# A hybrid decoder layer: v transposed on TensorE, the head's mean taken out on VectorE, and other figures in the list scheduler

## The chip, the cores and the metric

The kernel runs on one core of a Trainium2 chip. The core has five engines, each with its own instruction queue worked through in order: TensorE (PE in the profile; its weight loads are shown apart as PEld), VectorE (DVE), ScalarE (ACT), GpSimd (POOL) and SyncE (SP), which here issues all DMA transfers. PE writes to PSUM, whose banks hold 128 x 512 f32 each; POOL and DMA do not reach PSUM here. The metric is the device time of one execution in microseconds (us); lower is better.

## The reference

One layer of a decoder trunk with 4096 positions and a width of 1024. A normalised input is projected to the inputs of two groups of heads; both groups' outputs are gated, concatenated and projected back, then a residual and a final norm follow. The part that matters here is the second group, eight RWKV-7 heads of 64 channels.

```python
def _rwkv7_scan(r, decay, k, v, kk, a):
    def step(S, inp):
        r_t, w_t, k_t, v_t, kk_t, a_t = inp
        sa = jnp.einsum('bhvk,bhk->bhv', S, -kk_t)
        S = (S * w_t[:, :, None, :]
             + sa[..., None] * (kk_t * a_t)[:, :, None, :]
             + v_t[..., None] * k_t[:, :, None, :])
        y = jnp.einsum('bhvk,bhk->bhv', S, r_t)
        return S, y
...
    y = _rwkv7_scan(r_h, decay.reshape(hs), k_h, v_h, kk, a.reshape(hs))
    mu = jnp.mean(y, axis=-1, keepdims=True)
    var = jnp.mean(jnp.square(y - mu), axis=-1, keepdims=True)
    y = ((y - mu) * lax.rsqrt(var + RWKV_GN_EPS)).reshape(B, T, RWKV_W)
    y = y * rwkv_ln_w.astype(f32) + rwkv_ln_b.astype(f32)
    bonus = jnp.sum(r_h * k_h * rwkv_r_k.astype(f32), axis=-1, keepdims=True) * v_h
    rwkv_out = (y + bonus.reshape(B, T, RWKV_W)) * jax.nn.silu(rg)
```

The state is linear in v, row by row of the value dimension. So the mean of y over a head's 64 value channels is removed by removing the mean of v over those channels before the recurrence; the kernel does it there. The bonus uses v with its mean.

## The kernel before, in words

Activations lie with channels on the 128 partitions and time along the free axis, in eight blocks of 512 positions. The projections are f16 products: activations and weights are each split into a high and a low half, and three products of the halves are summed, so that a 128-channel output over 512 positions takes 24 products of 128 x 512.

Eight blocks times four pairs of heads make 32 **units**, numbered from 0. For each unit `rwkv_ab` projects k, r, v and the gate; builds decays; and makes the triangular products of eight chunks of 64 positions in two groups of four (tile `bank<-DD,bk` in the profile, a form that fills 64 of the 128 rows of the PE array). Masked copies put them into DD and Nb. For the inverse of the triangular factors, the 32 x 32 diagonal blocks of Nb go through DRAM (`nd`, then `f`), POOL makes 31 pairs of a product and a sum (`tm`, `Tc`), and the result returns through DRAM (`td`) into Nb. For the last unit DVE does that work. `rwkv_i` completes the 64 x 64 inverses with small products (`Ta`, `Nb`). `rwkv_c` runs the recurrence over the eight chunks: three products into the bank `ch`, with copies on ACT (`us`, `uv`) and the state's update on DVE (`sv`, `Sst`) between them. The output products go to the bank `y`, and `rwkv_d` scales them. DD and Nb have two buffers each, so the decay products of a unit wait until the recurrence two units earlier is done (`done["CC"] >= u - 1`).

At the end of `rwkv_ab`, v (channels by time) is brought to time by channels: four products per unit with the constant `c64` as the moving operand. `c64` holds identity minus 1/64 in a block for each head, so the product transposes and removes the head's mean at once. Four ACT copies take the bank into `sv`, which has two buffers.

The gated linear attention (`gla_lr`, `gla_proj`, `gla_pair`), the norm of the input (`x_block`), the splitting of weights in the first blocks (`split_w`, `split_o`) and the output projection (`out_block`, `out_last`) are further streams. Weights are split once, kept in DRAM (`wdr`) and loaded again for each block on the SP queue, together with every other transfer.

**The order** is made by the program. The streams are run against a model of the engines (`account`) that records every instruction as a `Step` with its duration, the delay until others see its result (`lag`) and its dependences (`put`). Then a list scheduler goes forward and backward over all steps (`forward`, `backward`) up to thirteen times and keeps the order with the smallest modelled end. The instructions are then issued to each engine's queue in that order, which the chip cannot change. The figures that stand in the model are these: a result is seen by another engine 0.2 us after its end (0.25 from PE), and by the same engine 0.075, 0.1 or 0.18 sooner (DVE, ACT, POOL); a DMA issue holds the SP queue for 0.63 us and its transfer starts 1.28 us after; a POOL instruction on n elements of two operands takes 0.14 + n x 2.13/960; a load's data are there 1.6 us after its transfer, plus `SPARE` of 0.45. Among the next twelve PE steps, one that keeps the form of the array tile (rows by columns) is preferred by 2.0 us over another, and a change of form is modelled with 0.09 us.

All instructions are recorded by one helper, so they all carry its line (L408) in the profile; they are told apart by their tiles.

Of the kernel before, what the change touches and what calls it, by code (L numbers as in the profile page):

```python
# [10 lines left out]
F32 = mybir.dt.float32  # L11
# [4 lines left out]
ALU = mybir.AluOpType  # L16
AX = mybir.AxisListType
PSUM = bass.MemoryType.PSUM
DRAM = bass.MemoryType.DRAM

P = 128
# [4 lines left out]
SPARE = 0.45  # L26
# [45 lines left out]
CK_C64 = 64  # L72
# [9 lines left out]
def hymba_kernel(ctx, tc, xT, wt, wg, wo, wua, gup, pk, ck, out):  # L82
# [5 lines left out]
    one = ctx.enter_context(tc.tile_pool(name="one", bufs=1))  # L88
# [14 lines left out]
    ready, used, busy = {}, {}, {}  # L103
# [59 lines left out]
    array = Array()  # L163

    def account(eng, out, ins, d, lag, cols=0, tiles=None):
        rdy = lambda k: (lambda r: r[0] - (r[1] == eng) * {"V": 0.075, "S": 0.1, "G": 0.18}.get(eng, 0.0))(ready.get(k, (0.0, "")))
        t = max([0.0] + [rdy(k) for a in ins for k in parts(a)]
                + [used.get(k, 0.0) for k in parts(out)]
                + [rdy(k) for k in parts(out) if eng != "T"])
        if eng == "T":  # L170
            t0, d = array.put(max(t, now[0]), d, cols, tiles)
            t, now[0] = t0, array.free
        else:
            if eng == "D":
                t0 = place("H", t, 0.63)
                t = t0 + 1.28
            t = place(eng, t, d)
            if eng != "D":
                t0 = t
        for a in ins:  # L180
            for k in parts(a):
                used[k] = max(used.get(k, 0.0), t + d + (0.95 if eng == "D" else 0.1))
        for k in parts(out):
            ready[k] = (t + d + lag, eng)
        return t0

    table = [0]
    steps, wkey, rkey, wlast, readers = [], {}, {}, {}, {}
# [22 lines left out]
    def put(t0, eng, d, lag, cols, tiles, tab, outs, ins, f):  # L211

        keys = lambda aps: {k: k in {y for x in aps for y in parts(x)} for a in aps for k in whole(a)}
        ki, ko = keys(ins), keys(outs)
        for k in list(ki) + list(ko):
            t0 = max(t0, wkey.get(k, 0.0))
        for k in ko:
            t0 = max(t0, rkey.get(k, 0.0))
        s = Step(len(steps), t0, eng, d, lag, cols, tiles, tab, f)
        got = lambda m: m.lag + SPARE * (m.eng == "D") - (m.eng == eng) * {"V": 0.075, "S": 0.1, "G": 0.18}.get(eng, 0.0)  # L220
        for k, timed in ki.items():
            rkey[k] = max(rkey.get(k, 0.0), t0)
            if k in wlast:
                s.follow(wlast[k], got(wlast[k]) if timed else None)
        for k, timed in ko.items():
            wkey[k] = t0
            if k in wlast:
                s.follow(wlast[k], got(wlast[k]) if timed and eng != "T" else None)
            for m in readers.get(k, ()):
                s.follow(m, (0.95 + SPARE if m.eng == "D" else 0.1) if timed else None)  # L230
            wlast[k], readers[k] = s, []
        for k in ki:
            if k not in ko:
                readers.setdefault(k, []).append(s)
        if eng == "T":

            if last[0] and last[1] == turn[0] and last[0].form == s.form != (4, 4):
                last[0].next = s
                s.follow(last[0], None)
            last[:] = [s, turn[0]]  # L240
        for m in s.on:
            m.to.append(s)
        steps.append(s)

    def forward(rank):


        wait, can, free = {e: [] for e in "VSGTD"}, {e: [] for e in "VSGTD"}, dict.fromkeys("VSGTDH", 0.0)
        pes, tab, run = Array(), 0, None
        left, ready, start = [len(s.on) for s in steps], [0.0] * len(steps), [0.0] * len(steps)  # L250
        end = [0.0] * len(steps)
        for s in steps:
            if not s.on:
                heapq.heappush(wait[s.eng], (0.0, s.n))

        def soonest(e):
            t = pes.free if e == "T" else free["H" if e == "D" else e]
            return t if can[e] else max(t, wait[e][0][0]) if wait[e] else 1e18

        for _ in steps:  # L260
            e = min("VSGTD", key=soonest)
            t = soonest(e)
            while wait[e] and wait[e][0][0] <= t:
                n = heapq.heappop(wait[e])[1]
                heapq.heappush(can[e], (rank[n], n))
            if e == "T":
                x = next((x for x in can[e] if run and x[1] == run.n), None)
                x = x or min(heapq.nsmallest(12, can[e]), key=lambda x: x[0] - 2.0 * (steps[x[1]].form == pes.form))
                run = steps[x[1]].next
                can[e].remove(x)  # L270
                heapq.heapify(can[e])
            else:
                x = can[e][0]
                soon = []
                while e in "VS" and wait[e] and wait[e][0][0] <= t + 0.15:
                    r, n = heapq.heappop(wait[e])
                    soon.append((r, n))
                    if rank[n] + 2 * (r - t) < x[0]:
                        x = (rank[n] + 2 * (r - t), n)
                for y in soon:  # L280
                    if y[1] != x[1]:
                        heapq.heappush(wait[e], y)
                if x is can[e][0]:
                    heapq.heappop(can[e])
            s = steps[x[1]]
            t, d = max(t, ready[s.n]), s.d
            start[s.n] = t
            if e == "T":
                start[s.n], d = pes.put(t, d, s.cols, s.tiles)
                end[s.n] = start[s.n] + d  # L290
            elif e == "D":
                free["H"], free["D"] = t + 0.63, max(t + 1.28, free["D"]) + d
                end[s.n] = free["D"]
            else:
                if s.tab is not None:
                    d, tab = d + 1.3 * (s.tab != tab), s.tab
                end[s.n] = free[e] = t + d
            for m in s.to:
                lat = m.on[s]
                ready[m.n] = max(ready[m.n], start[s.n] if lat is None or lat < 0 else end[s.n] + lat)  # L300
                left[m.n] -= 1
                if not left[m.n]:
                    heapq.heappush(wait[m.eng], (ready[m.n], m.n))
        return start, end

    def backward(end):
# [7 lines left out]
        for _ in steps:  # L314
            e = min("VSGTD", key=soonest)
            t = soonest(e)
            while wait[e] and wait[e][0][0] <= t:
                n = heapq.heappop(wait[e])[1]
                heapq.heappush(can[e], (-end[n], n))
            s = steps[heapq.heappop(can[e])[1]]  # L320
            hold = long = s.d
            if e == "T":
                hold, form = s.d * s.form[0] * s.form[1] / 16 + 0.09 * (s.form != form), s.form
            elif e == "D":
                hold, long = max(0.63, s.d), s.d + 1.28
            free[e], late[s.n] = t + hold, t + long
            for m, lat in s.on.items():
                ready[m.n] = max(ready[m.n], late[s.n] - m.d if lat is None or lat < 0 else late[s.n] + lat)
                left[m.n] -= 1
                if not left[m.n]:  # L330
                    heapq.heappush(wait[m.eng], (ready[m.n], m.n))
        return [-t for t in late]

    def cost(eng, op, ins, n, o, acc=False):
# [21 lines left out]
        if eng == "G":  # L356
            if op == "memset":
                return 0.135 + n * 0.52 / 960
            return 0.14 + 0.07 * few + n * (2.13 if len(big) > 1 else 0.95) / 960 + 0.34 * (n == 8)
        if n <= 4:  # L360
            return 0.1 if n == 1 else 0.03
        if n == 64 and o.shape[0] == 64:
# [4 lines left out]
    class Engine:  # L367
# [5 lines left out]
        def __getattr__(self, op):  # L373
            f = getattr(self.eng, op)

            def call(*a, **kw):
# [3 lines left out]
                if aps:  # L380
# [9 lines left out]
                        t0 = account("T", o, ins, d, lag, cols, tiles)  # L390
                    elif self.name == "D":
                        b = math.prod(o.shape) * (2 if o.dtype == F16 else 4)
                        d, lag = max(0.01, b / 3.6e5), 1.6 if ins[0].space == DRAM else 0.6
                        t0 = account("D", o, ins, d, lag)
                    else:
                        e = kw.get("accum_out")
# [84 lines left out]
    mc = sb(one, [P, P], U8, "mc")  # L481
    mg = sb(one, [P, P], U8, "mg")
    bones = sb(one, [P, 32], F32, "bones")
    c64 = sb(one, [P, P], F32, "c64")
    G.memset(c64, 0.0)
    smask = sb(one, [P, TB], U8, "smask")
    gmask = sb(one, [P, TB], U8, "gmask")
    sel = sb(one, [P, 4, 2], F32, "sel")
# [344 lines left out]
    def rwkv_ab(u, p, b, xs, LR):  # L833
# [125 lines left out]
        sv = sb(un, [P, NC, 2, 64], F32, "sv", 2)  # L959
        pv = (yield from need("r")).rearrange("p (c h t) -> p c h t", c=4, h=2)  # L960
        for c in range(4):
            T.matmul(pv[:, c], lhsT=v[:, P * c:P * c + P], rhs=c64, start=True, stop=True)

        for k, q in enumerate((lo, hi)):
            for e, o in enumerate((hi, lo)):
                S.copy(sv[o, k::2, e, :], pv[q, :, e, :])
# [378 lines left out]
    def setup():  # L1345
# [28 lines left out]
        for i, t in enumerate(("crs", "rgs")):  # L1374
# [5 lines left out]
            S.activation(uh[i], ur, AF.Copy, scale=usc[:, 2 * i:2 * i + 1])  # L1380
            V.scalar_tensor_tensor(ul[i][q], ur[q], usc[q, 2 * i:2 * i + 1], uh[i][q], ALU.mult, ALU.subtract)
            V.tensor_scalar_mul(usc[:, 4 + i:5 + i], usc[:, 2 * i + 1:2 * i + 2], 0.5 / 16384 if i == 0 else 0.5)
        for q in (slice(0, 64), slice(64, 128)):
            D.dma_start(c64[q, q], ck[q, CK_C64:CK_C64 + 64])


    units, invs_, hot = {}, {}, []
# [165 lines left out]
```

## Time and profile before

| what | value |
|---|---|
| device time, median of 3 runs | 2356.49 us (2355.05 to 2359.45) |
| device time of the profiled execution | 2357.35 us |
| its span, first to last instruction | 2355.5 us |
| mean granted PE clock | 0.979 |
| DMA moved | 322.13 MB on the hardware queue, 45.0% of 16 engines' span |

In the profile's groups, a line names the engine, the operation, the tile written and the tiles read, the shape, the count, then the busy time, the mean duration of one in ns and the idle time of the engine before it with what ended it. For PE the shape is rows*columns of the array, then the moving operand. Matmuls overlap in the pipeline, so the duration of one is not what it costs; the time from the start of a group to the start of the next is closer. In the list of waits, a row is who waited, for whom, the time in all, how often, and the longest.

### The profile page before, as it was taken

What the parts mean: (1) busy time and instruction counts of PE and PEld (TensorE: products, weight loads), DVE (VectorE), ACT (ScalarE), POOL (GpSimd) and SP (SyncE); (2) the same over time, 40 slices, a digit from 0 to 9 for tenths busy, and PEclk for the clock granted to TensorE, in tenths of its full rate; (3) what the DMA queues carried; (4) which work ended last, traced back from release to release, by engine and by line L of the source; (5) the groups of instructions that cost most, each with busy time, mean ns of one, the idle gap of its engine ahead of it and who ended that gap; (6) DMA issues with size and microseconds to landing.
All of it is one profiled execution on the core that took longest, in us unless ns stands there. A gap on an engine that the chain in (4) does not pass through costs nothing.

```text
span 2355.5 us, 52166 instructions
## 1 busy us (share of the span) xinstructions
PE 2245.6 (95%) x19432; PEld 1390.7 (59%) x19432; DVE 1664.7 (71%) x3737; ACT 1251.0 (53%) x3229; POOL 842.1 (36%) x2213
## 2 busy tenths in 40 slices
PE   6888999999999999999999999999999989999986
PEld 3556565556665666656575566655666556755643
DVE  7868768478764786757766787638877677676756
ACT  7566765454654655544654546535564455544442
POOL 3450333524334352235425342342514353321400
PEclk9989999999999999999999999999999999999989
DMA  6666545355334543345424553345533454334432
GB/s 195 204 217 213 158 154 157 113 169 152 103 106 125 179 151 93 109 137 174 141 85 121 175 160 97 102 133 173 153 94 106 123 184 137 97 118 127 130 86 76
DMA packets 275523, 325.46 MB, mean 138 GB/s; under 512 B 131732, under 2 KB 132932, under 8 KB 275268
## 3 DMA queue, kind: packets, MB, share of 16 engines
q1 hardware_dynamic: 275268, 322.13, 45.0%
q8 instruction: 152, 2.49, 0.4%
q14 instruction: 103, 0.84, 0.1%
HBM read 276.97 MB, written 45.05 MB: 137 GB/s over the span
## 4 chain that ended last, share of the span: by engine, by line
PE 68%; DVE 19%; DMA 5%; issue 3%; ACT 2%; POOL 2%; SPq 1%; DVEq 0%; ACTq 0%; POOLq 0%
PE bank L408 60%; PE ch L408 6%; PE y L408 2%; DVE DD L408 2%; DVE nta L408 2%; DVE bk L408 1%; POOL tm L408 1%; POOL Tc L408 1%; DVE mgg L408 1%; DVE mgr L408 1%; SPq L408 1%; DMA wdr<-wo 1%; DVE Nb L408 1%; DVE crs L408 1%; DVE sv L408 1%
## 5 line engine op out<-in xcount | busy, mean ns | idle before, releaser
L408 PE MATMUL bank<-x,wr 128*128 128x512 f16 x3264 | 803.1, 380 | 12.5 <-DVE rk L408 4.7
L408 POOL TENSOR_TENSOR tm<-Tc,f 128x60 f32<-128x60 f32 (+24 forms) x961 | 332.4, 346 | 762.3 <-DMA f<-nd 586.0
L408 PEld LDWEIGHTS <-wr 128*128 128x128 f16 x3264 | 317.0, 100 | 308.0 <-issue 21.4
L408 PE MATMUL bank<-x,wg 128*128 128x512 f16 x1536 | 389.6, 383 | 2.4 <-DMA wg<-wdr 2.0
L408 POOL TENSOR_TENSOR Tc<-Tc,tm 128x60 f32<-128x60 f32 (+24 forms) x961 | 341.6, 355 | 73.4
L408 PE MATMUL bank<-x,wo 128*128 128x512 f16 x1488 | 361.9, 384 | 0.6 <-ACT bk L408 0.6
L408 DVE SCALAR_TENSOR_TENSOR sv<-ch,PC,psd 64x64 f32<-64x64 f32 x448 | 126.2, 282 | 195.9 <-PE ch L408 191.0
L408 POOL TENSOR_TENSOR xacc<-xacc,xr 128x512 f32<-128x512 f32 x98 | 131.3, 1340 | 314.8 <-ACT xr L408 215.3
L408 PEld LDWEIGHTS <-wg 128*128 128x128 f16 x1536 | 148.5, 101 | 147.4 <-issue 11.6
L408 PEld LDWEIGHTS <-wo 128*128 128x128 f16 x1488 | 146.0, 101 | 139.9 <-issue 8.0
L408 PEld LDWEIGHTS <-x 128*128 128x128 f16 x3120 | 189.9, 100 | 27.6 <-issue 12.2
L408 PE MATMUL bank<-wg,x 128*128 128x128 f16 x3072 | 199.6, 222 | 4.5 <-DMA wg<-wdr 4.5
L408 ACT ACTIVATE psd<-sv,PC 128x128 f32<-128x128 f32 x256 | 102.2, 399 | 190.1 <-DVE sv L408 152.9
L408 ACT COPY uv<-ch 64x64 f32<-64x64 f32 x512 | 105.5, 206 | 120.5 <-PE ch L408 114.8
L408 ACT COPY us<-ch 64x64 f32<-64x64 f32 x512 | 105.3, 206 | 103.7 <-PE ch L408 93.3
L408 PEld LDWEIGHTS ch<-sv,DD 128*128 128x128 f32 x512 | 91.9, 192 | 49.3 <-DVE sv L408 20.3
L408 PEld LDWEIGHTS ch<-us,Nb 128*128 128x128 f32 x512 | 92.3, 192 | 40.0 <-ACT us L408 10.5
L408 PEld LDWEIGHTS ch<-uv,bk 128*128 128x128 f32 x512 | 92.4, 192 | 39.6 <-ACT uv L408 12.5
L408 PE MATMUL ch<-sv,DD 128*128 128x128 f32 x512 | 105.9, 289 | 8.7 <-DVE sv L408 6.6
L408 ACT ACTIVATE sa<-bank,mu_s 128x512 f32<-128x512 f32 x104 | 71.5, 688 | 73.5 <-PE bank L408 68.5
L408 PE MATMUL ch<-uv,bk 128*128 128x128 f32 x512 | 103.4, 284 | 4.1 <-ACT uv L408 4.0
L408 POOL MEMSET Tc<- 32x8 f32 (+1 forms) x160 | 23.7, 148 | 223.3 <-DMA td<-Tc 182.2
(332 smaller groups left out, 3670.9 us busy)
## 6 DMA issues: line engine op xcount, KB each, us to landing
wr<-wdr SPq DMA_DIRECT2D x256, 256.0 KB
wg<-wdr SPq DMA_DIRECT2D x184, 256.0 KB
xr<-in_xT_dram SPq DMA_DIRECT2D x176, 256.0 KB
wo<-wdr SPq DMA_DIRECT2D x128, 256.0 KB
f<-nd SPq DMA_DIRECT2D x128, 128.0 KB
x<-in_wt_dram SPq DMA_DIRECT2D x29, 512.0 KB
wdr<-wo SPq DMA_DIRECT2D x25, 512.0 KB
out_dram<-mgg SPq DMA_DIRECT2D x33, 256.0 KB
```

The lines of the kernel that those rows point to most:

```text
L408: put(t0, self.name, d, lag, cols, tiles, tab, outs, ins, lambda: f(*a, **kw))
```

## The change

The four products of v with `c64` become four transposes against the identity; the mean of each head is then reduced on DVE and subtracted in PSUM in place, before the ACT copies. `c64` and its loads go. In the model, a new function `early` shortens the delays between engines, the DMA figures change, `forward` holds back a transfer while eight are in flight, a POOL instruction takes 0.09 us more, and the preference for the present tile form falls from 2.0 to 0.5.

```diff
     def account(eng, out, ins, d, lag, cols=0, tiles=None):
-        rdy = lambda k: (lambda r: r[0] - (r[1] == eng) * {"V": 0.075, "S": 0.1, "G": 0.18}.get(eng, 0.0))(ready.get(k, (0.0, "")))
+        rdy = lambda k: (lambda r: r[0] + early(r[1], eng))(ready.get(k, (0.0, "")))
...
             if eng == "D":
-                t0 = place("H", t, 0.63)
-                t = t0 + 1.28
+                t0 = place("H", t, 0.5)
+                t = t0 + 1.15
...
+    def early(a, b):
+
+        if a not in "VSGT" or b not in "VSGT" or not a:
+            return 0.0
+        if a == b:
+            return {"V": -0.075, "S": -0.1, "G": -0.18, "T": 0.0}[a]
+        return -0.045 if a == "T" else -0.09 if b == "T" else -0.07
...
-        got = lambda m: m.lag + SPARE * (m.eng == "D") - (m.eng == eng) * {"V": 0.075, "S": 0.1, "G": 0.18}.get(eng, 0.0)
+        got = lambda m: m.lag + SPARE * (m.eng == "D") + early(m.eng, eng)
...
-        end = [0.0] * len(steps)
+        end, flight = [0.0] * len(steps), []
...
-                x = x or min(heapq.nsmallest(12, can[e]), key=lambda x: x[0] - 2.0 * (steps[x[1]].form == pes.form))
+                x = x or min(heapq.nsmallest(12, can[e]), key=lambda x: x[0] - 0.5 * (steps[x[1]].form == pes.form))
...
             elif e == "D":
-                free["H"], free["D"] = t + 0.63, max(t + 1.28, free["D"]) + d
+                if len(flight) > 7:
+                    start[s.n] = t = max(t, flight[-8])
+                free["H"], free["D"] = t + 0.5, max(t + 1.15, free["D"]) + d
                 end[s.n] = free["D"]
+                flight.append(end[s.n] + s.lag)
...
-                hold, long = max(0.63, s.d), s.d + 1.28
+                hold, long = max(0.5, s.d), s.d + 1.15
...
-            return 0.14 + 0.07 * few + n * (2.13 if len(big) > 1 else 0.95) / 960 + 0.34 * (n == 8)
+            return 0.23 + 0.07 * few + n * (2.13 if len(big) > 1 else 0.95) / 960 + 0.34 * (n == 8)
...
-                        d, lag = max(0.01, b / 3.6e5), 1.6 if ins[0].space == DRAM else 0.6
+                        d = max(0.01, b / 3.6e5)
+                        if ins[0].space == DRAM:
+                            lag = {"wdr": 1.1, "in": 1.9 if b > 4e5 else 1.1, "td": 1.2}.get(ins[0].tensor.name.split("_")[0].rstrip("0123456789"), 1.7)
+                        else:
+                            lag = 2.1 if b > 2e5 else 1.2 if o.shape[-1] == 32 else 0.6
...
-    c64 = sb(one, [P, P], F32, "c64")
-    G.memset(c64, 0.0)
...
         for c in range(4):
-            T.matmul(pv[:, c], lhsT=v[:, P * c:P * c + P], rhs=c64, start=True, stop=True)
-
+            T.transpose(pv[:, c].rearrange("p h t -> p (h t)"), v[:, P * c:P * c + P], ident)
+        vm = sb(rt, [P, 8, 1], F32, "vm", 1)
+        pu = pv.rearrange("p c h t -> p (c h) t")
+        V.tensor_reduce(vm, pu, op=ALU.add, axis=AX.X)
+        V.scalar_tensor_tensor(pu, vm.broadcast_to((P, 8, 64)), -1.0 / 64, pu, ALU.mult, ALU.add)
         for k, q in enumerate((lo, hi)):
...
-        for q in (slice(0, 64), slice(64, 128)):
-            D.dma_start(c64[q, q], ck[q, CK_C64:CK_C64 + 64])
```

## The prediction

> **What bounds the kernel now.** I read the page first: span, engines, the clock row, the chain that ended last. Then a table of stretches, to see where TensorE (PE) is short of work.
>
> ```profile
> span 2355.5 us, 52166 instructions
> PE 2245.6 (95%) x19432; PEld 1390.7 (59%) x19432; DVE 1664.7 (71%) x3737; ACT 1251.0 (53%) x3229; POOL 842.1 (36%) x2213
> PE 68%; DVE 19%; DMA 5%; issue 3%; ACT 2%; POOL 2%; SPq 1%; DVEq 0%; ACTq 0%; POOLq 0%
> ```
>
> ```profile
> 59.00:118.00 59.00, 51.73 (x419) 33.98 (x419) 52.24 (x118) 33.08 (x61) 25.84 (x35) 0.92 0.66 203
> 118.00:177.00 59.00, 49.83 (x372) 31.03 (x369) 41.06 (x125) 35.86 (x73) 33.59 (x97) 0.88 0.69 219
> 295.00:2242.00 1947.00, 1909.37 (x16755) 1188.10 (x16750) 1360.51 (x2917) 1016.75 (x2706) 736.85 (x1967) 0.99 0.44 133
> 2242.00:2356.00 114.00, 85.53 (x683) 49.19 (x681) 67.97 (x188) 38.97 (x117) 0.00 (x0) 0.86 0.26 79
> 1180.00:1239.00 59.00, 59.00 (x662) 41.79 (x660) 38.98 (x90) 30.04 (x84) 18.27 (x53) 1.00 0.29 86
> ```
>
> The columns are the stretch, its length, busy time of PE, weight load, VectorE (DVE), ScalarE (ACT) and GpSimd (POOL), the granted clock, the DMA share and GB/s. From 295 to 2242 us PE is busy for 1909 of 1947 us, at a clock of 0.99: this long middle is PE-bound, with 37.6 us of waiting in all, and DVE has 30% of it free (1360 of 1947). Before 295 us weights are split and DVE is as full as PE (52.2 of 59 in one stretch). After 2242 us the last unit's recurrence runs as a chain of latencies. So PE work taken out counts in the middle, and there nearly in full. The waits of PE in that middle, longest first:
>
> ```profile
> PE bank L408 <- DVE bk L408: 8.1, 8, 3.3
> PE bank L408 <- DMA wg<-wdr: 4.5, 3, 2.9
> ...
> PE ch L408 <- DVE sv L408: 2.3, 5, 0.8
> PE ch L408 <- DVE Sst L408: 1.8, 1, 1.8
> ...
> PE ch L408 <- ACT uv L408: 1.2, 2, 0.9
> PE bank L408 <- DMA wr<-wdr: 1.2, 1, 1.2
> ...
> PE ch L408 <- ACT us L408: 0.9, 2, 0.5
> ```
>
> No cause stands out. The recurrence (tile ch) costs 2.3 + 1.8 + 1.2 + 0.9 = 6.2 us, late weights 5.7 us in four waits.
>
> **The v transpose on PE.** Before, each unit multiplies four 128-column pieces of v by c64. These are f32 matmuls, and each runs as two passes: 128 calls show as 256 instructions in all, 224 of them (28 units) in the middle. The transposes of bk are the form that v gets now; they run as one instruction each.
>
> ```profile
> L408 PE MATMUL bank<-ident,bk 128*128 128x128 f32 x232 | 34.5, 277 | 2.2 <-DVE DD L408 2.2
> ...
> L408 PE MATMUL bank<-c,v 128*128 128x128 f32 x224 | 32.4, 278 | 0.0
> ```
>
> ```profile
> 1193.20 0.59 PE L408 MATMUL bank<-x,wr 128*128 128x512 f16 x2
> 1193.72 1.16 PE L408 MATMUL bank<-DD,bk 64*128 64x128 f32 x16
> ...
> 1199.96 1.11 PE L408 MATMUL bank<-c,v 128*128 128x128 f32 x8
> 1200.91 0.81 PE L408 MATMUL bank<-x,wr 128*128 128x512 f16 x3
> ...
> 1206.92 0.82 PE L408 MATMUL bank<-ident,bk 128*128 128x128 f32 x6
> 1207.58 0.39 PE L408 MATMUL ch<-sv,DD 128*128 128x128 f32 x2
> ```
>
> From start to start, the eight passes of one unit hold PE for 1200.91 - 1199.96 = 0.95 us; six transposes hold it for 0.66 us, or 0.11 each. Four transposes then take 0.44, and a unit gives back 0.51 us. Over the 28 units of the middle that is **14.3 us**. The bounds: 112 passes fewer at 0.11 give 12.3; by busy time, 32.4 less 112 x 34.5/232 = 16.7 leaves 15.7. The four units outside the middle I count at nothing, since PE waits there anyway.
>
> **The mean on DVE.** Two instructions per unit are new: a reduction over 512 PSUM elements, and a three-operand pass that reads and writes PSUM. The nearest rows:
>
> ```profile
> L408 DVE TENSOR_REDUCE amW<-bank 128x1 f32<-128x128 f32 x33 | 9.5, 287 | 26.6 <-PE bank L408 26.3
> L408 DVE TENSOR_REDUCE amW<-rgs 128x1 f32<-128x512 f32 x1 | 0.7, 677 | 0.0
> L408 DVE SCALAR_TENSOR_TENSOR v<-bank,omu_s,sa 128x512 f32<-128x512 f32 x40 | 29.9, 747 | 16.5 <-ACT sa L408 15.7
> L408 DVE SCALAR_TENSOR_TENSOR rgs<-rgs,bank 128x512 f32<-128x512 f32 x32 | 21.9, 683 | 28.1 <-ACT rgs L408 27.8
> L408 DVE SCALAR_TENSOR_TENSOR r<-r,pkt,kf 128x512 f32<-128x512 f32 x32 | 26.2, 818 | 0.1
> ```
>
> I take 0.68 for the reduction (same length, from SBUF; four of the PSUM one would be 1.15) and 0.75 for the pass (0.68 to 0.82; no row shows DVE writing PSUM). That is 1.43 us a unit, 1.36 to 1.97, and 46 us over 32 units. In the middle its cover is DVE's free 586 us, 21 us a unit. What it delays is the four ACT copies into sv, by 1.5 us and whatever DVE is busy with. They have this much time:
>
> ```profile
> 1201.11 1.50 ACT L408 COPY sv<-bank 64x256 f32<-64x256 f32 x4
> ...
> 1264.08 0.38 PE L408 MATMUL ch<-sv,DD 128*128 128x128 f32 x2
> ...
> 2134.56 1.50 ACT L408 COPY sv<-bank 64x256 f32<-64x256 f32 x4 [5.57 <-PE bank L408]
> ...
> 2136.56 0.38 PE L408 MATMUL ch<-sv,DD 128*128 128x128 f32 x2
> ```
>
> Unit 16 reads sv some 61 us after the copies end; unit 29 only 0.5 us after. So the delay is hidden where the order keeps such a distance, and a unit like 29 starts its recurrence a microsecond late, behind which PE has projections to run. Value in the middle: 0. Without that cover it is up to 28 x 1.43 = 40 us, which is a rival below. Before 295 us three units fall where DVE is 70 to 90% full: between 0 and 3 x 1.43 = 4.3, I take +2.1. At the end, DVE computes the last unit's inverse itself, back to back, in the same microseconds as the last v product:
>
> ```profile
> 2237.63 0.19 DVE L408 TENSOR_TENSOR tm<-Tc,f 128x31 f32<-128x31 f32 x1 [2.88 <-DMA bcdb<-brow]
> ...
> 2252.20 0.83 PE L408 MATMUL bank<-c,v 128*128 128x128 f32 x6
> ...
> 2256.71 0.17 DVE L408 TENSOR_TENSOR Tc<-Tc,tm 128x8 f32<-128x8 f32 x1
> ```
>
> The last chain hangs on that inverse, so two more DVE passes inside it cost +1.4 (0 if they are placed behind it). ACT's copies and the PSUM bank are held 1.5 us longer per unit; the other five banks turn meanwhile, so nothing is counted. The dropped memset and two small loads of c64 are at the start, off the path.
>
> **The order.** Every instruction is placed by a list scheduler from the figures in the code, and four kinds of them change. First, the hand-over between engines gets 0.045 to 0.09 us shorter. Second, a POOL step gets 0.09 longer:
>
> ```profile
> 1216.65 0.24 POOL L408 TENSOR_TENSOR tm<-Tc,f 128x31 f32<-128x31 f32 x1 [42.67 <-DMA f<-nd]
> 1216.97 0.25 POOL L408 TENSOR_TENSOR Tc<-Tc,tm 128x31 f32<-128x31 f32 x1
> ```
>
> The step takes 0.32 us from start to start; the old figures give 0.14 + 31 x 2.13/960 + 0.02 = 0.23, the new ones 0.32. Over the 62 steps of an inverse the old order expected the result 5.6 us too soon, and whatever it placed behind it stood too early in the queues. Third, a DMA issue goes from 0.63 to 0.50, with at most eight transfers in flight and a delay for each kind. The trace has issues of 0.32 and 0.57:
>
> ```profile
> 1199.99 0.32 SPq L408 DMA_DIRECT2D wr<-wdr  x1
> ...
> 1220.92 0.57 SPq L408 DMA_DIRECT2D bcdb<-brow  x1
> ```
>
> Each of these three lies nearer to the trace, so PE should wait less for things that come late. The bounds are wide: all 37.6 us of the middle's waits (not more, PE has nothing else to give) to a loss of as much. I take a sixth, **-6**, because the largest single cause (DVE bk, 8.1) isn't one that a corrected figure removes. Fourth, the preference for staying with one tile form falls from 2.0 to 0.5 us, so PE changes form more often. A change costs 0.09: two f16 products of 0.216 would end at 1193.63, and the 64-row group starts at 1193.72. A unit has about ten small-tile groups; if a quarter of 32 x 10 groups lose a neighbour that is 80 changes or 7 us, if none 0. I take +2, since most such groups already stand alone among 512-column products, as the group of 16 at 1193.72 does.
>
> **The sum**: 2355.5 - 14.3 + 2.1 + 1.4 - 6 + 2 = 2340.7 us of span. The profiled execution took 2357.35 us, 1.85 over its span, and stands 0.86 above the median of the runs, 2356.49. So 2340.7 + 1.85 - 0.86 = **2341.7 us**, 0.6% faster.
>
> **Rivals.**
> (a) *The order gains more.* With half of the middle's waits gone (18.8 instead of 6) the time is 2329. For it: three figures err in the same direction now. Against: 98% busy leaves only small pieces.
> (b) *The small terms all fall at their bad ends*: form changes 7, start 4.3, order 0. That is 13 us more, 2355, no change that can be told.
> (c) *Transposes run at half clock and save nothing.* Four at 0.22 take 0.88 of the old 0.95; 2 us are left of 14.3, and the time is 2354. Against it: the stretch 1180 to 1239 holds a unit's eight transposes, at 0.11 each, at a granted clock of 1.00. The Trainium skill, page "TensorE: Matmul & The Clock Gate", section "Part 4: PE-mode transpose", says that transposes don't count as PE activity for the clock gate, so that the full clock doesn't engage for them. By that rule the clock would sink where they stand; the trace disagrees as long as they stand among products, which four of them do.
> (d) *Slower: the recurrence loop becomes the bound.* A unit's decay products may start only when the recurrence two units earlier is done, and DVE serves both. Where PE runs out of other work, a unit loses DVE's 1.43 and the saved 0.51 is worth nothing. It decides from eight units on (8 x 1.94 = 15.5, the gain); in half of the 28 it costs 27 us, 2369. For it: the pass sits in an in-order queue. Against: ch waits of 6.2 us show that PE has had filler nearly always.
> (e) *Slower: loads come too late.* The new figures make loads short, so the order may issue them just in time on the one SP queue, behind instructions that wait. Four such waits cost 5.7 us now; sixteen more of 1.4 us cost 23, 2365; from ten on the gain is gone. Against: the cap of eight in flight pulls the other way.
>
> **How the numbers follow.** Forecast 54%, (a) 22%, (b) 7%, (c) 3%, (d) 7%, (e) 7%. About 0.2% (4.7 us) is what a measurement of this kernel tells from none, so faster is below 2351.8 and slower above 2361.2: 76% faster, 10% the same, 14% slower. The forecast's own range is 2331 to 2352. The whole range goes down past (a), to where three quarters of the middle's waits are gone (28.2 instead of 6) and forms cost nothing (2 more), 2318, and up to (e), 2364; about 8% lies below, 10% above.
>
> **What would show it.** The group bank<-c,v is gone and bank<-ident,v stands at 128 instructions of about 0.11 us each; PE's busy time is some 17 us lower. DVE has 46 us more, in rows near 0.68 and 0.75. In the middle PE stays at 97% or more; waits on DMA and ch don't grow past about 12 us; the clock there stays at 0.99. The forecast is wrong if ch or weight loads lead PE's waits, if the clock sinks near the transposes, or if the last unit's products start no earlier than now.

## The result, and the profile after

| | before | after |
|---|---|---|
| device time, median of 12 runs each | 2359.01 us (2355.05 to 2366.77) | 2357.75 us (2352.66 to 2363.67) |
| span of the profiled execution | 2355.5 us | 2356.1 us |
| mean granted PE clock | 0.979 | 0.986 |

The ratio is 0.9993 [0.9983, 1.0004]: no difference that can be told. The time lies inside the predicted range, but 0.7% above the forecast, and the gain that was put at 76% didn't come. First the head of the page after and two rows of its table of stretches (columns as in the prediction):

```profile
span 2356.1 us, 52042 instructions
...
PE 2232.6 (95%) x19304; PEld 1360.3 (58%) x19304; DVE 1716.6 (73%) x3801; ACT 1251.8 (53%) x3229; POOL 869.0 (37%) x2212
```

```profile
0.00:295.00 295.00, 245.24 (x1906) 146.24 (x1907) 234.50 (x628) 192.66 (x394) 106.46 (x245) 0.95 0.63 197
295.00:2242.00 1947.00, 1901.66 (x16702) 1165.08 (x16700) 1411.23 (x2975) 1019.22 (x2717) 762.58 (x1967) 1.00 0.44 133
```

PE's busy time fell by 13.0 us (2245.6 to 2232.6) and the span didn't, so PE is idle 13.6 us more. In the middle its idle time went from 37.6 to 45.3 us (1947 - 1901.66). The parts of the change are there, in the groups of the middle, of the whole trace, and in the timeline of one unit:

```profile
L423 PE MATMUL bank<-ident,v 128*128 128x128 f32 x112 | 18.6, 275 | 0.5 <-ACT brow L423 0.5
```

```profile
L423 DVE SCALAR_TENSOR_TENSOR bank<-vm,bank 128x512 f32<-128x512 f32 x32 | 22.2, 695 | 0.9
...
L423 DVE TENSOR_REDUCE vm<-bank 128x8 f32<-128x512 f32 x32 | 21.9, 686 | 5.0 <-PE bank L423 4.6
```

```profile
812.79 0.61 PE L423 MATMUL bank<-ident,v 128*128 128x128 f32 x4
813.24 1.24 PE L423 MATMUL bank<-x,wr 128*128 128x512 f16 x5
```

Four transposes hold PE for 0.45 us; the mean costs DVE 0.686 + 0.695 us. What PE waited for in the middle, longest first (who, for whom, time, times, longest):

```profile
PE ch L423 <- ACT uv L423: 7.0, 7, 1.9
PE bank L423 <- DMA wg<-wdr: 5.4, 3, 3.4
PE ch L423 <- DVE sv L423: 5.1, 5, 1.5
```

The recurrence now leads. A second list of the same kind shows it far better: what the weight loads (PEld) waited for in the middle. Each product has such a load ahead of it. A wait here is idle time of the loads, and not all of it is lost to PE: between two f16 products the loads idle some 0.12 us anyhow (a load takes 0.10 us, and the products start 0.216 us apart). Before, then after (rows without a tile and rows of other operands left out):

```profile
PEld ch L408 <- DVE sv L408: 12.5, 26, 1.3
...
PEld ch L408 <- ACT uv L408: 6.9, 21, 1.1
...
PEld ch L408 <- ACT us L408: 4.4, 10, 1.0
...
PEld bank L408 <- DVE Ta L408: 3.5, 9, 0.4
```

```profile
PEld ch L423 <- ACT us L423: 19.7, 81, 0.9
PEld ch L423 <- ACT uv L423: 19.3, 39, 2.4
PEld ch L423 <- DVE sv L423: 17.3, 33, 2.0
PEld bank L423 <- DVE Ta L423: 14.8, 28, 2.0
```

The three operands of the recurrence went from 23.8 us in 57 waits to 56.3 us in 153, the 64 x 64 inverses (Ta) from 3.5 to 14.8. To see whether this can hold the lost gain, I set each matmul's distance to the next one, start to start, against the shortest usual distance of its form (216 ns for 512 f16 columns, 109 for 128 f32 columns, both on the full array). What lies above that is put down to one cause each (a sixth, neighbours of f32 and f16, is 17 us in all three and left out). The rows are estimates: where a distance has two causes, the split is a choice, and another one moves a row by some 3 us:

| us of the whole span | before | after | f4 (below) |
|---|---|---|---|
| the matmuls at their usual distance | 2010.8 | 1996.8 | 1996.8 |
| longer waits (over 0.35 us, or recorded) | 124.2 | 140.6 | 139.4 |
| short slips (0.03 to 0.35 us) | 21.4 | 28.5 | 23.7 |
| change of the array tile's form | 74.5 | 77.8 | 73.4 |
| small tiles | 54.6 | 57.8 | 55.4 |
| at a lowered clock | 38.0 | 22.8 | 41.7 |

The work shrank by 14.0 us, which the forecast had right. Longer waits took 16.4, slips 7.1, forms and small tiles 6.5; a clock that sank less gave 15.2 back. That clock goes with the order, as the runs below show: the mean granted clock was 0.982 to 0.986 over the runs of the new order with the old v (f2), 0.977 to 0.983 with the new v's transposes in the old order (f4), and 0.975 to 0.983 in before.

### The profile page after: what moved, and what is told of

Same layout as the page of the kernel before. It is cut to its first block, busy times and chain, and to the rows that moved or that the text cites. A ratio compares the mean times of both kernels' runs of the same rounds, so it can differ in the third digit from the quotient of the medians.

```text
span 2356.1 us, 52042 instructions
## 1 busy us (share of the span) xinstructions
PE 2232.6 (95%) x19304; PEld 1360.3 (58%) x19304; DVE 1716.6 (73%) x3801; ACT 1251.8 (53%) x3229; POOL 869.0 (37%) x2212
## 3 DMA queue, kind: packets, MB, share of 16 engines
q1 hardware_dynamic: 275108, 322.10, 45.3%
## 5 line engine op out<-in xcount | busy, mean ns | idle before, releaser
L423 POOL TENSOR_TENSOR tm<-Tc,f 128x60 f32<-128x60 f32 (+24 forms) x961 | 348.9, 363 | 645.2 <-DMA f<-nd 512.4
L423 PE MATMUL bank<-x,wg 128*128 128x512 f16 x1536 | 376.0, 381 | 1.0 <-DVE wo L423 0.5
L423 POOL TENSOR_TENSOR Tc<-Tc,tm 128x60 f32<-128x60 f32 (+24 forms) x961 | 348.3, 362 | 73.6
L423 PEld LDWEIGHTS ch<-uv,bk 128*128 128x128 f32 x512 | 89.7, 190 | 50.1 <-ACT uv L423 24.7
L423 PEld LDWEIGHTS ch<-sv,DD 128*128 128x128 f32 x512 | 89.6, 190 | 50.1 <-DVE sv L423 23.5
L423 PEld LDWEIGHTS ch<-us,Nb 128*128 128x128 f32 x512 | 85.9, 190 | 45.2 <-ACT us L423 27.3
L423 ACT ACTIVATE sa<-bank,mu_s 128x512 f32<-128x512 f32 x104 | 71.6, 688 | 73.1 <-PE bank L423 71.9
```

Of the source, the lines that this page charges most:

```text
L423: put(t0, self.name, d, lag, cols, tiles, tab, outs, ins, lambda: f(*a, **kw))
```

## The experiments

In the diffs of f1 to f5 and of e1 and e2, `hook` names what is issued in place of a planned instruction: the plan, and so the order of all queues, stays that of the kernel it is taken from. In the other runs the scheduler plans anew. Ratios, with their 95% intervals, are to runs of the kernel before that were taken along with each experiment (medians from 2359.55 to 2361.08 us, but 2359.01 for after), so they say more than the times.

### The new v in the old order, and the old v in the new order

f1 keeps the order of before. The reduction and the pass are issued on DVE just ahead of the first copy into sv.

```diff
-T.matmul(pv[:, c], lhsT=v[...], rhs=c64, ...)
+T.matmul(pv[:, c], lhsT=v[...], rhs=c64, ..., hook=lambda f, a, kw: nc.tensor.transpose(pv[:, c]..., v[...], ident))
-S.copy(sv[o, k::2, e, :], pv[q, :, e, :])
+S.copy(sv[o, k::2, e, :], pv[q, :, e, :], hook=mean_first)   # first of four
+def mean_first(f, a, kw):
+    nc.vector.tensor_reduce(vm, pu, op=ALU.add, axis=AX.X)
+    nc.vector.scalar_tensor_tensor(pu, vm.broadcast_to((P, 8, 64)), -1.0 / 64, pu, ALU.mult, ALU.add)
+    f(*a, **kw)
```

> The order of before on every queue, with v transposed by transposes and the mean taken out on DVE just ahead of the ACT copies; c64 is loaded but not read. Theory H (the new instructions save what was forecast, and the new order loses it, because its shorter hand-over to PE puts the recurrence's products into PE's queue before us, uv and sv are there): about 13 us under before, 2344 to 2347. Theory D (the two DVE passes delay what PE waits for and take the gain back, whatever the order): within 4 us of before, 2354 to 2361.

f2 is the reverse: the order of after, with the products of c64 and nothing in the place of the two DVE passes.

```diff
-T.transpose(pv[:, c]..., v[...], ident)
+T.transpose(..., hook=lambda f, a, kw: nc.tensor.matmul(pv[:, c], lhsT=v[...], rhs=c64, ...))
-V.tensor_reduce(vm, pu, ...)
+V.tensor_reduce(vm, pu, ..., hook=lambda f, a, kw: None)
```

> The new order on every queue, with the old products of v with c64 and no mean on DVE. Theory H: some 13 us over before, 2368 to 2373, because the order alone is worse. Theory D: 2356 to 2362; PE has 14 us more work than in the new kernel but DVE's passes no longer delay it.

f1 took 2392.74 us, 1.0131 [1.0114, 1.0149], above what either theory gave; f2 2365.89 us, 1.0017 [1.0006, 1.0028], between the two. The new order with the old v costs 4 us. In it the new v is worth some 6 us (1.0017 against 0.9993), while in the old one it costs 31. The waits of the weight loads in f2's middle show that most of their growth comes with the new order, with the old v too (50.1 us for the three operands, and Ta as in after):

```profile
PEld ch L424 <- ACT us L424: 20.6, 75, 1.3
PEld ch L424 <- DVE sv L424: 15.3, 28, 2.0
PEld bank L424 <- DVE Ta L424: 14.8, 28, 1.7
PEld ch L424 <- ACT uv L424: 14.2, 33, 1.3
```

What ACT waited for in f1, over the whole span, has a row that before doesn't have, and after has it small (the tile vm's list of who waited for it):

```profile
ACT sv L971 <- DVE bank L970: 59.9, 31, 7.0
```

```profile
  ACT sv L423: 16.2, 15
```

ACT's queue stands 31 times behind DVE, up to 7.0 us, with us and uv queued behind the copies. f5 moves only those four copies, 2.5 us later in ACT's queue but no later than their first reader.

```diff
-for s in sorted(steps, key=lambda s: (start[s.n], s.n)):
+# the four copies: min(start[s.n] + 2.5, start of the first reader)
```

> The order of before with the new v as in the first run, but the four ACT copies into sv stand 2.5 us later in ACT's queue (or just ahead of their first reader, where that is sooner). Theory A (the first run lost its time in ACT's queue: the copies waited for DVE there, with the recurrence's copies us and uv behind them): 2350 to 2362. Theory B (the two passes delay the recurrence's updates of sv in DVE's own queue): 2380 to 2392 as before.

2377.35 us, 1.0074 [1.006, 1.0087], between the theories: moving the copies gives back some 14 of f1's 31 us. ACT still stands behind DVE at these copies, less often:

```profile
ACT sv L409 <- DVE bank L970: 42.8, 24, 7.0
```

So what remains comes with the two passes (f4 below, without them, is level with before), but whether through ACT's queue or through DVE's own was not divided.

### The mean alone, and the PE time alone

f3 is after without the two passes (the mean of v is not removed).

```diff
-V.tensor_reduce(vm, pu, ...)
+V.tensor_reduce(vm, pu, ..., hook=lambda f, a, kw: None)
...
+V.scalar_tensor_tensor(..., hook=lambda f, a, kw: None)
```

> The new kernel in the same order, with the mean of v left out: the transposes stay, the two DVE passes of each unit are not issued. Theory H: within 4 us of the new kernel, 2354 to 2360, since DVE has room. Theory D: 10 us or more under the new kernel, 2342 to 2347.

2356.5 us, 0.9985 [0.9973, 0.9997], as theory H has it. Where the passes are planned for, they cost some 2 us, which is not clear of noise: the intervals of f3 and after overlap.

f3 against f2 is the PE time alone, in the new order: both have that order and neither has the two passes, but f2 has the products with c64 and f3 the transposes. The ratio falls from 1.0017 to 0.9985, by intervals that don't meet. **In the new order 14 us of PE work taken out are worth 7.5 us, about half.** The weight loads wait as long for the three operands in f3 (50.9 us) as in f2 (50.1).

f4 is f1 without the two passes: before's order, PE's work 14 us smaller, nothing added on any engine (the mean of v is not removed here either).

```diff
 def mean_first(f, a, kw):
-    nc.vector.tensor_reduce(...)
-    nc.vector.scalar_tensor_tensor(...)
     f(*a, **kw)
```

> The order of before, with v transposed by transposes and the mean of v left out: PE has 14 us less to do, and nothing else changes in any queue. Theory P (PE sets the time in the middle, as the prediction had it): 2346 to 2350, 10 us or more under before. Theory Q (an order that is fixed turns most of the time saved into waits for the recurrence and the inverse, which come no sooner): 2353 to 2359.

2358.64 us, 0.9996 [0.9987, 1.0006], as theory Q has it: **14 us of PE work taken out of before's order, at no cost elsewhere, is worth nothing there.** Its row of the middle, then the weight loads' waits there:

```profile
295.00:2242.00 1947.00, 1900.01 (x16637) 1173.26 (x16637) 1358.40 (x2902) 1014.77 (x2705) 732.11 (x1967) 0.99 0.46 132
```

```profile
PEld ch L409 <- DVE sv L409: 19.8, 37, 2.2
...
PEld ch L409 <- ACT uv L409: 11.0, 30, 1.1
...
PEld ch L409 <- ACT us L409: 7.1, 18, 1.2
```

The three waits sum to 37.9 us against 23.8, and PE's idle time in the middle grows from 37.6 to 47.0. In the table above, longer waits rise by 15.2, the work falls by 14.0. That fits theory Q: PE reaches the recurrence's products sooner and stands in front of operands that come no sooner. (The table and the rows are of f4's profiled execution, whose 2365.0 us lie 6.4 us above the median, so its waits are somewhat longer than usual.) Why the same work counts for half in the new order and for nothing in this one stays open.

### The model's figures, one by one

The scheduler plans these anew: u1 takes out the shorter hand-over between engines, u2 restores the preference for the present form, u3 the POOL step; a has the new v with all old figures, b the old v with all new ones.

```diff
-        return -0.045 if a == "T" else -0.09 if b == "T" else -0.07
+        return 0.0                                    # u1
...
-0.5 * (steps[x[1]].form == pes.form)
+2.0 * (steps[x[1]].form == pes.form)                  # u2
...
-return 0.23 + 0.07 * few + ...
+return 0.14 + 0.07 * few + ...                        # u3
```

> The new kernel with the old hand-over between engines in the model (a result is seen by another engine 0.2 us after its end, 0.25 from PE); all else new, and planned anew. Theory H: PE's short waits for us, uv, sv and Ta go back to what before had, 2342 to 2348. Theory D: 2354 to 2361. A planned order may also move by a few us by itself.

> The new kernel with the preference for the present tile form back at 2.0, planned anew. Theory R: fewer changes of form (some 3 us of PE's time) and more reserve, 2347 to 2354. Theory S: 2354 to 2360, no change that can be told.

> The new kernel with the POOL step's old figure (0.14), planned anew: the inverse is expected 5.6 us too soon again. Theory R: slower, 2360 to 2370, since a figure that is too short takes reserve away. Theory S: about the same, 2355 to 2362.

> The new v (transposes, mean on DVE, no c64) planned anew with every old figure of the model. Theory R (the new v brings its 13 us wherever DVE's passes are planned for; the new figures lose it again, because what they take off the plan is reserve that the chip needs): 2340 to 2348. Theory S (PE work taken out brings at most about 6 us in any order, as in the run with the new order and the old v, because the recurrence loop comes up beside PE): 2350 to 2357.

> The old v (products with c64) planned anew with every new figure of the model. Theory R: slower than before by about as much as the new v brings, 2366 to 2373. Theory S: 2358 to 2366.

A new plan moves instructions in every queue. To know what such a move is worth by itself, four runs change a figure by a hundredth, which means nothing for the chip: `SPARE` (0.45 to 0.46) and `DP` (0.15 to 0.16), which sets the place of the gated-attention projections among the streams, in before (j1, j2) and in after (j3, j4).

```diff
-SPARE = 0.45
+SPARE = 0.46          # j1, j3
...
-DP = 0.15
+DP = 0.16             # j2, j4
```

> The kernel before with one figure of its model a hundredth of a microsecond off (SPARE, what is added to a load's delay, 0.46 for 0.45), planned anew; no instruction differs, only the order. Theory L (the order of before stands at the good end of a wide spread that its model gives, because two wrong figures of it only just cancel): 2365 to 2385. Theory N (the spread is a few us, and it is the new figures that lose the gain): 2353 to 2361.

> The kernel before with another figure a little off (DP, the place of the gated-attention projections among the streams, 0.16 for 0.15), planned anew. Theory L: 2365 to 2385. Theory N: 2353 to 2361.

> The new kernel with SPARE 0.46 for 0.45, planned anew. Theory L (its figures agree with the chip, so its orders lie closer together): 2352 to 2364. Theory N: 2354 to 2361.

> The new kernel with DP 0.16 for 0.15, planned anew. Theory L: 2352 to 2364. Theory N: 2354 to 2361.

Theory D has u1 and theory S has u2; u3, a and b took longer than any range gave. Theory L has j1 and j2; j3 and j4 took longer than either theory gave. The last column is the end that the scheduler's own model reaches for the order that it issues.

| version | time, us | ratio to before | span | planned end |
|---|---|---|---|---|
| before | 2359.01 | 1 | 2355.5 | 2331.9 |
| after | 2357.75 | 0.9993 [0.9983, 1.0004] | 2356.1 | 2316.7 |
| u1 old hand-over | 2356.41 | 0.9983 [0.9973, 0.9994] | 2354.3 | 2325.1 |
| u2 form 2.0 | 2359.97 | 1.0 [0.9986, 1.0014] | 2358.9 | 2330.7 |
| u3 POOL 0.14 | 2412.22 | 1.0211 [1.019, 1.0233] | 2418.7 | 2307.9 |
| a new v, old model | 2376.16 | 1.0067 [1.0047, 1.0088] | 2373.9 | 2310.6 |
| b old v, new model | 2379.84 | 1.0071 [1.0057, 1.0086] | 2380.4 | 2337.2 |
| j1 before, SPARE | 2382.74 | 1.0087 [1.0068, 1.0106] | 2380.9 | 2334.5 |
| j2 before, DP | 2367.52 | 1.0026 [1.0014, 1.0037] | 2365.5 | 2313.7 |
| j3 after, SPARE | 2369.17 | 1.0034 [1.0018, 1.0049] | 2366.3 | 2320.3 |
| j4 after, DP | 2383.93 | 1.0098 [1.0073, 1.0122] | 2383.4 | 2323.7 |

Three readings. **First**, meaningless changes cost 0.26% and 0.87% on before and 0.41% and 1.05% on after: both kernels stand at the good end of a spread of some 6 to 25 us (two changes each, so its size is rough). Runs a and b lie in that spread, so they say nothing of the parts, and nothing shows that the new figures narrowed it. **Second**, the plan's end doesn't order the versions: from before to after it promised 15.2 us, and the chip gave nothing; the best of the plans, u3, is the slowest. **Third**, u3 lies outside the spread, at twice its largest step. Between the start of the transfer of Nb to DRAM and the finished Nb, units 3 to 30 take on average, planned and traced:

| us per unit | path planned | path traced | inverse alone planned | inverse alone traced |
|---|---|---|---|---|
| before | 71.6 | 71.5 | 23.8 | 27.9 |
| after | 75.5 | 75.9 | 29.7 | 30.2 |
| u3 | 68.9 | 72.1 | 23.3 | 27.7 |

Before's model had POOL 4.1 us too fast and the rest of the path about as much too slow, and the whole was right to 0.1 us. The change corrects both. u3 corrects the transfers but not POOL, and each unit's Nb is finished 3.2 us later than planned. These paths hold waits in the queues as well, so their agreement in before doesn't show that the errors cancel (e1 below leaves 9.3 us of the inverse out, and the path is as long). PE's largest wait in u3's middle is another than in after, where it is 5.4 us:

```profile
PE bank L423 <- DMA wg<-wdr: 22.1, 6, 6.8
```

That the late inverses hold up these loads on the one SP queue would fit, but it wasn't tried alone, and before has SP waiting for POOL as long.

### Is it the inverse's path that sets the pace?

e1 is before's order with the last 20 of the 62 POOL steps of each inverse left out (not those of the last unit), so the inverses are not complete; e2 is e1 with f4's edit. In e1's trace the inverse of units 3 to 30 takes 18.6 us instead of 27.9, which is 9.3 us less and more than the 6.5 expected.

```diff
+skip = dict(hook=lambda f, a, kw: None) if j >= 21 and E is G else {}
 E.tensor_tensor(tm..., Tc..., F..., ALU.mult, **skip)
 E.tensor_tensor(Tc..., Tc..., tm..., ALU.add, **skip)
```

> The order of before on every queue, with the last 20 of the 62 POOL steps of each inverse (but the last unit's) left out, some 6.5 us of each unit's path from its products to its recurrence. Theory L (this path and the recurrence, not PE's work, set the pace): at least 12 us faster, 2300 to 2346. Theory P (PE sets the pace and the path has slack): within 5 us of before, 2354 to 2361.

> As the run with the short inverse, and v transposed by transposes with the mean of v left out (14 us less PE work). Theory L: with the path shorter PE's work counts, 8 to 14 us under the run with the short inverse alone. Theory P: the same distance as without the short inverse, 0 to 3 us.

e1 took 2339.15 us, 0.9904 [0.9887, 0.9922], inside theory L's range; e2 2333.18 us, 0.9884 [0.9863, 0.9905], 6 us under e1 and between its theories. The first stretch of before, two stretches of e1, and the list of e1's transfers of Nb to DRAM, with the first and the last start (before's last one starts at 2229.2):

```profile
0.00:295.00 295.00, 250.69 (x2008) 153.44 (x2010) 236.21 (x634) 195.33 (x406) 105.25 (x246) 0.93 0.63 197
```

```profile
0.00:295.00 295.00, 258.47 (x2176) 159.54 (x2177) 246.92 (x662) 201.51 (x422) 82.31 (x186) 0.96 0.66 203
295.00:2242.00 1947.00, 1906.01 (x16687) 1185.07 (x16684) 1361.97 (x2957) 1018.22 (x2716) 535.67 (x1407) 0.99 0.46 132
```

```profile
L409 SPq DMA_DIRECT2D nd<-Nb x128: 302/423/1562, 77.2 to 2203.8; - x128
```

The gain of 18 us of span falls mostly in the start: 168 matmuls more than before are through by 295 us (x2176 against x2008), and the triangular products of unit 3 begin 13.4 us earlier. The timeline of before, then of e1:

```profile
293.70 0.48 PE L408 MATMUL bank<-DD,bk 64*128 64x128 f32 x2
```

```profile
280.30 0.49 PE L409 MATMUL bank<-DD,bk 64*128 64x128 f32 x2
```

From unit 3 to unit 30 the lead at the first transfer of Nb stays between 13.4 and 17.8 us (16.9 at unit 30); at the last transfer of the last unit it is 25.4, at the end 18. So a shorter inverse speeds up the start. Of the middle e1 says little, because there it didn't shorten the path: from the start of the transfer of Nb to the finished Nb, units 3 to 30 took 71.3 us against 71.5, although the inverse in it was 9.3 us shorter. The result's transfer back (`td`) was issued 4.0 us sooner after the transfer of Nb, and its data were back in Nb only 0.4 us sooner. That fits queues whose order is held: what stands behind the inverse comes when its turn comes. e2 against e1, 0.2% with intervals that overlap, doesn't tell whether the PE time counts once the inverse is short. What paces the middle of a held order stays open, beyond that PE stands before the recurrence's operands.

## Why the prediction was wrong, point by point

From before through f2 and f3 to after, the measured 0.07% (1.7 us) falls into three steps: the new order costs 4 us, the PE work taken out in it gives 7.5, the mean on DVE costs 2. Two terms of the sum failed.

- **PE passes, -14.3: the size of the work was right** (14.0 in the table of distances, 0.45 us for four transposes against 0.44), **the step that failed is the sentence before it**: "So PE work taken out counts in the middle, and there nearly in full." In before's order it counts for nothing (f4, 0.9996 [0.9987, 1.0006]), in the new order for about half (f3 against f2, 7.5 us). The prediction read 98% busy as PE-bound, and took 6.2 us of recurrence waits as proof of spare work. The weight loads had waited 23.8 us for the same operands.
- **Order, -6, and form changes, +2: the second failed term.** Forecast were 4 us gained, and the new order with the old v (f2) is 0.17% slower, 4 us. The middle has 584 instead of 540 changes of form, by 0.093 us each 4 us, twice the forecast. The six were a choice inside bounds of 37.6 either way, with no row behind it: in place of shorter waits, f2 has the recurrence's loads wait 50.1 us instead of 23.8, and the better clock, which the prediction put at no change, made up for a part. Why figures that lie nearer the trace gave such an order stays open. What a single figure brings can't be said: the runs that plan anew differ by no more than their spread, but for u3.
- **DVE's mean, 0 in the middle: right for an order that plans it.** Duration 1.38 us instead of 1.43; f3 puts its cost at some 2 us, not clear of noise. The price without cover, up to 40 us, was about right too: f1 against f4 is 1.0131 against 0.9996, 32 us.
- **Start and end, +2.1 and +1.4**: at the end, the last unit's reduction starts at 2261.1 us, just as its inverse on DVE ends, so the two passes don't lie inside the inverse. But the unit's triangular products begin at 2218.6 us instead of 2214.0, no earlier, which the prediction named as a sign that it is wrong; the other, that ch leads PE's waits, is there too. In the start, up to 295 us, PE is busy for 245.2 us in after and for 248.8 in f3, which has the same order without the two passes. As far as one execution each can show it, the mean costs 3.6 us there, inside the 0 to 4.3 that the prediction gave.
- **Rival (c), half clock, is refuted**: four transposes take 0.45 us, and the granted clock of the middle is 1.00 in after and 0.99 in f4 as in before. The Trainium skill, page "TensorE: Matmul & The Clock Gate", section "Part 4: PE-mode transpose", says that the full clock doesn't engage for transposes; here they ran at the full clock among products, and what a long run of transposes alone would do no run here shows.
- **Rival (e), late loads, is refuted**: PE waited 5.4 and 1.6 us for wg and wr, against 4.5 and 1.2.
- **Rival (d), the recurrence as the bound, came nearest**, at a smaller price: in before's order the saved 0.51 us per unit was worth nothing, as it says, but DVE's 1.43 was not lost on top in the new one. That it comes about by decay products which wait for the recurrence two units earlier was not tested. It was given 7%. That the time came out near rival (b), 2355, is chance: the order without gain and 4 of its 7 us of forms were there, but (b) kept the whole 14.3 us of the PE passes.

## What to carry to other kernels

An engine that is busy for 98% of a stage is not thereby its bound: read the waits of its weight loads too, and ask of each unit whether its operands would come any sooner if the engine were faster. A run that takes the work out and holds every queue's order (f4) answers that for this order before anything is planned anew; another order can give another answer (f3 against f2). Such a held order can also hide what a shorter step would free (e1: 9.3 us less inverse, and a path as long as before). Where a scheduler writes the order, change a figure by a hundredth first to see its spread (here up to 1%), and don't expect that a figure nearer to the trace gives a faster order (u3, 2.1% slower with the transfers corrected and POOL not).

## What the runs showed of the hardware

A product that waits for a late operand holds its weight load back too, even where the load doesn't need that operand. The groups of after, the loads and then the products of us with Nb, and the loads in before:

```profile
L423 PEld LDWEIGHTS ch<-us,Nb 128*128 128x128 f32 x512 | 85.9, 190 | 45.2 <-ACT us L423 27.3
```

```profile
L423 PE MATMUL ch<-us,Nb 128*128 128x64 f32 x512 | 92.8, 263 | 3.7 <-ACT us L423 2.9 <-ACT Nb L423 0.5
```

```profile
L408 PEld LDWEIGHTS ch<-us,Nb 128*128 128x128 f32 x512 | 92.3, 192 | 40.0 <-ACT us L408 10.5
```

What is loaded, 128x128, is a block of Nb; us, 128x64, is what the product streams. Nb is finished before the first of these products of its unit, yet it is the load that waits for the copy of us (27.3 us in after, the products 2.9). The load takes 190 ns, nearly as long as a product of 512 f16 columns (216 ns from start to start). Whether it could be let run ahead of the copy was not tried. Between engines a waiting instruction starts far sooner after its producer's end than either model had it: medians of 34 to 39 ns between DVE, ACT and PE's results (whose ends are modelled by the profile), 53 ns for a matmul. And a reduction of 512 PSUM elements on DVE (686 ns) costs as much as a pass that reads and writes them (695 ns).
